# Up projection: rounded weights' products ahead of the remainders', no column shift of its weights, and 74 remainders built by ACT and an accumulating transfer that POOL issues

## The chip, the cores and the metric

The kernel runs on one core of one Trainium2 chip. The metric is the device time of one execution in microseconds (us), median of several runs. The engines are named as in the profile: PE (TensorE, matmuls), PEld (TensorE's weight loads, which run beside the matmuls), DVE (VectorE), ACT (ScalarE), POOL (GpSimd) and SP (SyncE, which issues most transfers).

## The reference

Two layers of a bidirectional encoder over 256 tokens of width 2048. The part that the change touches is the feed-forward half of a layer:

```
h2 = rms_norm(x, ln2_g[l])
u = depthwise_conv(h2 @ w_up[l], conv_w[l], conv_b[l])   # w_up: 2048 x 11264, conv over 3 positions
gate, up = u[..., :D_FF], u[..., D_FF:]                  # D_FF = 5632
x = x + (jax.nn.silu(gate) * up) @ w_down[l]
```

Ahead of it stand a projection of 2048 to 4608 columns, two kinds of attention and an output projection. All is in float32.

## The kernel before, in words

**Numbers in two parts.** A float32 product is made of three products of a shorter format (fp32r) that PE takes at full rate. A weight w is split by `split` (L109): ACT rounds it into `whi` (L112), and DVE subtracts, w - whi, into the remainder `wlo` (L113). The tokens are split in the same way into `xs[k]`, a tile of 2 x 256 columns with the rounded tokens in the first 256 and their remainders in the last 256. One long matmul of 512 columns, whi against both parts of `xs[k]`, gives two of the products; one short matmul of 256 columns, wlo against the rounded tokens alone, gives the third. The product of the two remainders is left out.

**The up projection.** Here the weights are the stationary operand (128 x 128, loaded anew for every matmul) and the tokens are the moving one. For each of the 44 groups `f` of 128 gate and 128 up columns the 16 slices `k` of 128 rows are summed in PSUM. The weights of a group come as two quanta `u` of 1 MB (128 x 2048), each worked in two half blocks of 128 x 1024. A half block holds 4 slices k for both sides j (gate and up), so it has 8 pairs of a long and a short matmul. `q_up` (L527) goes over j and k and calls `two` (L411), which issues the long matmul and at once the short one of the same pair. Two layers have 2 x 44 x 4 = 352 half blocks and 2816 pairs.

**Everywhere else** (input projection, output projection, down projection) the roles are swapped: tokens or activations are stationary, `whi` and `wlo` move with 512 columns, and `three` or `q_seven` issue the matmuls. Part of the down projection (kind "seven") uses a scheme with seven products, and its weights get some additions on DVE before they are split.

**Places in SBUF.** A tile `const` of 48 columns, `SHIFT`, sets where all later tiles begin. The tiles `whi` and `wlo` are 1024 + 64 columns wide; the up projection's weights lie in them from column 56 on (`UP_AT`, L53 and L756), all others from column 0. By the built program all of `xs`, `mid` (activations), `whi` and `wlo` begin at 96 bytes past a multiple of 256 bytes. So for the up projection the weights stand 224 bytes out of line with the tokens, and everywhere else the two are in line.

**What sets the order.** The work is a list of quanta. `load` (L735, its transfer is issued at L741) brings a quantum's raw weights by SP into one of three `raw` buffers; the next load into a buffer is issued when its last half was split. `split_w` (L752) splits a half block four steps ahead of its use (SPLIT_AHEAD), into one of five pairs of buffers. So the split of a half block can begin when the one five steps ahead of it has been multiplied, and it has four half blocks of time. A list scheduler then places the instructions of each engine; splits have a raised priority.

After a group's last half block `glu` (L543 to L563) takes the sums out of PSUM and makes the convolution, the gate and the product: on ACT L545, L555, L559, on DVE L546, L547, L557, L561, on POOL two copies of a halo (L549, L550), and then a split of the result into `mid` (L112, L113). For the seven products `sums_mid` adds more of it.

Of the kernel before, what the change touches and what calls it, by code (L numbers as in the profile page):

```python
# [12 lines left out]
F32R = mybir.dt.float32r  # L13
I32 = mybir.dt.int32
AF = mybir.ActivationFunctionType
ALU = mybir.AluOpType
AX = mybir.AxisListType

P = 128
# [4 lines left out]
KD = D // P  # L24
# [24 lines left out]
SPLIT_AHEAD = 4  # L49
AHEAD_PRIO = 40  # L50
SHIFT = 48

UP_AT = 56  # L53
WARM = 14

SPARE = 3 * (("qT", 3),)
# [3 lines left out]
def encoder_kernel(  # L60
# [5 lines left out]
    nc = tc.nc  # L66
    const = ctx.enter_context(tc.tile_pool(name="const", bufs=1))
    wp = ctx.enter_context(tc.tile_pool(name="wp", bufs=2))
# [28 lines left out]
    def mm(ps, lhsT, rhs, start, stop):  # L97
        nc.tensor.matmul(ps, lhsT, rhs, start=start, stop=stop, skip_group_check=True)  # L98
# [27 lines left out]
    xs = {}  # L126
# [276 lines left out]


    quanta = []
    side = {}

    def at(q, f, *args, half=1):
        side.setdefault((q, half), []).append((f, args))

    def two(ps, w_h, w_l, mv, first, last):  # L411

        mm(ps, w_h, mv, first, False)
        mm(ps[:, 1], w_l, mv[:, 0], False, last)

    def three(ps, terms, hv, lv, first, last, apart=False):

# [16 lines left out]
    def q_win(l, j, u):  # L434
        def body(q, half, hi, lo):
            ps = banks("in", u == 0 and half == 0)
            hv, lv = (w.rearrange("p (k n) -> p k n", k=2) for w in (hi, lo))
            k = 4 * u + 2 * half
            three(ps, (xs[k], xs[k + 1]), hv, lv, k == 0, k == KD - 2)
            if half == 0:  # L440
                return
            if u == 0 and j == 0 and l > 0:
                load_qk_g(l)
            if u == 2 and j == 1:
                rope_tables(l)
            if u == 3:
                if l == 0 and j == 0:
                    at(q + 4, done_win, q, l, j, ps, half=0)
                else:
                    done_win(q, l, j, ps)  # L450
        return body
# [38 lines left out]
    def q_wout(l, grp, nb, u):  # L490
        def body(q, half, hi, lo):
            g = 0 if grp == "a" else 1
            ps = banks("out", u == 0 and half == 0)
            hv, lv = (w.rearrange("p (k n) -> p k n", k=2) for w in (hi, lo))
            h = 4 * u + 2 * half
            three(ps, (os[g * NH + h], os[g * NH + h + 1]), hv, lv, h == 0, h == NH - 2)
            if nb == 0 and u == 0 and half == 1:
                stat_o(grp)
            if u == 1 and half == 1:
                if grp == "b":  # L500
                    add_x(nb, ps, st["ro"])
                else:
                    whole_x(q, l, 1, nb, ps, st["ro"])
        return body
# [22 lines left out]
    def q_up(l, f, u):  # L527
        def body(q, half, hi, lo):
            if u == 0 and half == 0:
                cur["up"] = psum.tile([P, 2, 2, T], F32, name="mm", bufs=2)  # L530
            ps = cur["up"]
            hv, lv = (w.rearrange("p (k j n) -> p k j n", k=4, j=2) for w in (hi, lo))
            for j in range(2):
                for kk in range(4):
                    k = 8 * u + 4 * half + kk
                    two(ps[:, j], hv[:, kk, j], lv[:, kk, j], xs[k], k == 0, k == KD - 1)
            if u == 1 and half == 1:
                glu(l, f, ps)
        return body

    def glu(l, f, ps):
        ux = halo[f % 2]
        r = T // GRID_W  # L543
        t = work.tile([P, 2, T], F32, name="prob", bufs=2)
        nc.scalar.activation(t, ps[:, :, 0], AF.Copy)  # L545
        nc.vector.tensor_add(t, t, ps[:, :, 1])  # L546
        nc.vector.tensor_mul(ux[:, :, r:r + T], t, st["r2"][:, None, :].to_broadcast([P, 2, T]))  # L547

        nc.gpsimd.tensor_copy(ux[:, :, 1:r], ux[:, :, T:T + r - 1])  # L549
        nc.gpsimd.tensor_copy(ux[:, :, T + r:T + 2 * r - 1], ux[:, :, r + 1:2 * r])  # L550
        y = work.tile([P, 2, T], F32, name="pT", bufs=4)
        for j in range(2):
            c = j * NF + f
            w0, w1, w2, b = (par["conv"][:, l, i, c:c + 1] for i in range(4))
            nc.scalar.activation(y[:, j, :], ux[:, j, r:r + T], AF.Identity, scale=w1, bias=b)  # L555
            for w, o in ((w0, 0), (w2, 2 * r)):
                nc.vector.scalar_tensor_tensor(y[:, j, :], ux[:, j, o:o + T], w, y[:, j, :],  # L557
                                               op0=ALU.mult, op1=ALU.add)
        nc.scalar.activation(t[:, 0, :], y[:, 0, :], AF.Silu)  # L559
        m = work.tile([P, T], F32, name="bias", bufs=2)  # L560
        nc.vector.tensor_mul(m, t[:, 0, :], y[:, 1, :])  # L561
        gs[f] = middle(l, f)
        split(gs[f][:, 0], gs[f][:, 1], m)  # L563
        ms[f] = m
        if f % 2 and f < NF - CHUNKS[-1] + PART:
            sums_mid(l, f // 2, ms.pop(f - 1), ms.pop(f))
# [132 lines left out]
    for l in range(L):  # L699
        for j in range(NJ):  # L700
            for u in range(4):
                quanta.append((a["w_in"][l, j, u], q_win(l, j, u), ""))
        for grp in "ba":
            for nb in range(NB):
                for u in range(2):
                    quanta.append((a["w_out"][l, 0 if grp == "a" else 1, nb, u], q_wout(l, grp, nb, u), ""))
        f = 0
        for c, nf in enumerate(CHUNKS):
            up = lambda f: [(a["w_up"][l, f, u], q_up(l, f, u), "up") for u in range(2)]
            down = lambda nb, g: [(a["w_down"][l, sum(CHUNKS[:c]) // FG + g, nb], q_down(l, c, nb, g), "")]  # L710
            seven = lambda i: [(a["w_seven"][l, c, i], q_seven(l, c, i), "seven")]

            end = sum(CHUNKS[:c]) + PART + 1
            while f < end:
                quanta += up(f)
                f += 1
            quanta.append((a["w_plain"][l, c], q_plain(l, c), ""))
            if nf == PART:
                for i in range(PAIRS):
                    quanta += seven(i) + down(2 + i // 2, i % 2)  # L720
            else:

                for i in range(PAIRS):
                    quanta += seven(i)
                    if f < NF:
                        quanta += up(f)
                        f += 1
                for nb, g in ((2, 0), (2, 1), (2, 2), (0, 2), (3, 0), (1, 2), (3, 1), (3, 2)):
                    quanta += down(nb, g)


    steps = [(q, h) for q in range(len(quanta)) for h in range(3 if quanta[q][2] == "seven" else 2)]
    raw, hl, left, loads, highs = {}, {}, {}, {}, {}

    def load(q, parts=1):  # L735
        if q < len(quanta):
# [6 lines left out]
    def split_seven(w, part, hi, lo):  # L743

        hv, lv = (t.rearrange("p (k n) -> p k n", k=2) for t in (hi, lo))
        if part == 1:
            nc.vector.tensor_sub(w[:, 1:3], w[:, 1:3], w[:, 2:4])
            nc.vector.tensor_add(w[:, 3], w[:, 3], w[:, 1])
            nc.vector.tensor_sub(w[:, 0], w[:, 3], w[:, 0])
        return split(hv, lv, (w[:, 1::2], w[:, 1:3], w[:, 0::3])[part])  # L750

    def split_w(s, parts=1):  # L752
        if s < len(steps):
            q, half = steps[s]
            kind = quanta[q][2]
            o = UP_AT if kind == "up" else 0  # L756
            hl[s] = tuple(wp.tile([P, 1024 + 64], F32R, name=t, bufs=SPLIT_AHEAD + 1)[:, o:o + 1024]
                          for t in ("whi", "wlo"))
            with tc.high_priority(offset=AHEAD_PRIO if s >= KD // 2 else 0):
                if kind == "seven":  # L760
                    highs[s] = split_seven(raw[q].rearrange("p (k n) -> p k n", k=4), half, *hl[s])
                else:
                    m = 1024 // parts
                    for j in range(parts):
                        highs[s] = split(*(t[:, j * m:(j + 1) * m] for t in hl[s]),
                                         raw[q][:, half * 1024 + j * m:half * 1024 + (j + 1) * m])
            left[q] -= 1
            if left[q] == 0:
                del raw[q]
                load(q + LOAD_AHEAD)  # L770
# [61 lines left out]
    ps = psum.tile([P, T], F32, name="pv", bufs=1)  # L832
# [3 lines left out]
    for i in range(SPLIT_AHEAD):  # L836
        first_x(i)
        split_w(i, 2 if i == 0 else 1)
# [122 lines left out]
```

## Time and profile before

| | |
|---|---|
| median of 3 runs | 2092.17 us (2092.07 to 2092.38) |
| the profiled execution: its time | 2092.0 us |
| its span | 2090.2 us |
| PE busy | 2083.5 us, 10816 matmuls |
| DVE busy | 1720.5 us |
| ACT busy | 1222.3 us |
| POOL busy | 170.3 us |
| moved by the transfers | 408.42 MB, 195 GB/s in the mean |

The profile is one execution with the start and the length of every instruction. Its page has, among others, the busy time of each engine, the chain of work that ended last (followed back from the end, at each step to what released it), and groups of like instructions with their count, their busy time and the mean of one. The timeline lists instructions in order of time; like ones that follow each other stand in one row with their count, and the time of such a row runs from the first one's start to the last one's end. Matmuls overlap: the next begins before the last has ended. So what one of them costs is read from start to start, not from its length.

### The profile page before, as it was taken

The page shows a single profiled execution, that of the slowest core. Times are in us where ns is not written, and L with a number is a line of the kernel's source. Part 1 is how long each engine was busy: PE and PEld are TensorE (multiplying, and loading weights), DVE is VectorE, ACT ScalarE, POOL GpSimd, SP SyncE. Part 2 cuts the span into 40 slices and gives each one's busy share as a digit, 9 for nine tenths or more (in the row PEclk, how much of TensorE's full clock was granted, in tenths as well). Part 3 has the DMA queues.
Part 4 walks back from the last instruction along what each step waited for, and adds up shares of the span by engine and source line. Part 5 has one row for each costly group of instructions (what it writes and reads, how often), then busy time and mean ns, then how long its engine had stood idle before and what let it go on. Part 6 is the DMA issues. An engine that isn't in the chain of part 4 may idle for free.

```text
span 2090.2 us, 29185 instructions
## 1 busy us (share of the span) xinstructions
PE 2083.5 (100%) x10816; PEld 1789.2 (86%) x10816; DVE 1720.5 (82%) x2604; ACT 1222.3 (58%) x1817; POOL 170.3 (8%) x237
## 2 busy tenths in 40 slices
PE   9999999999999999999999999999999999999999
PEld 8888888888888888888888888888888888888887
DVE  7786757898898988989757866678989989899896
ACT  7566556555555556556555665565556555555563
POOL 0011100100101001010000011001001010010100
PEclk9999999999999999999999999999999999999999
DMA  9544555556565564655655444555555655556554
GB/s 350 199 145 164 179 172 174 198 195 211 180 241 182 208 210 167 242 193 211 208 181 181 162 160 166 177 182 189 214 202 170 236 199 204 201 185 234 185 200 161
DMA packets 62144, 408.42 MB, mean 195 GB/s; under 512 B 7344, under 2 KB 9904, under 8 KB 13744
## 3 DMA queue, kind: packets, MB, share of 16 engines
q1 hardware_dynamic: 61280, 405.46, 56.2%
q8 instruction: 85, 1.39, 0.3%
q10 hardware_dynamic: 720, 1.08, 0.2%
q14 instruction: 59, 0.48, 0.1%
HBM read 404.42 MB, written 2.10 MB: 194 GB/s over the span
## 4 chain that ended last, share of the span: by engine, by line
PE 99%; DMA 0%; ACT 0%; DVE 0%; issue 0%
PE mm L98 90%; PE S L98 4%; PE pv L98 3%; PE tr L98 2%; PE tr L373 1%; PE tr L307 1%; PE S L149 1%; DMA head<-in_head 0%; ACT qtok L274 0%; ACT kT L315 0%; ACT xs L115 0%; DVE x L688 0%; ACT whi L112 0%
## 5 line engine op out<-in xcount | busy, mean ns | idle before, releaser
L112 ACT ACTIVATE whi<-raw 128x1024 fp32r<-128x1024 f32 (+1 forms) x797 | 830.9, 1057 | 689.9 <-PE mm L98 411.9
L113 DVE TENSOR_TENSOR wlo<-raw,whi 128x1024 fp32r<-128x1024 f32 (+1 forms) x797 | 963.9, 1220 | 270.3 <-ACT whi L112 231.8
L98 PE MATMUL mm<-xs,whi 128*128 128x512 f32 x2816 | 977.0, 390 | 0.0
L98 PE MATMUL mm<-xs,wlo 128*128 128x256 f32 x2816 | 794.1, 282 | 0.0
L98 PEld LDWEIGHTS mm<-xs,whi 128*128 128x128 f32 x2816 | 528.3, 188 | 110.5
L98 PEld LDWEIGHTS mm<-xs,wlo 128*128 128x128 f32 x2816 | 532.2, 189 | 1.1
L98 PE MATMUL mm<-whi,mid 128*128 128x512 f32 x1412 | 368.2, 391 | 0.0
L98 PEld LDWEIGHTS mm<-whi,mid 128*128 128x128 f32 x1412 | 263.0, 188 | 53.9
L98 PE MATMUL mm<-whi,xs 128*128 128x512 f32 x1152 | 294.2, 393 | 1.4 <-ACT qtok L274 1.3
L98 PEld LDWEIGHTS mm<-whi,xs 128*128 128x128 f32 x1152 | 213.1, 188 | 44.7 <-ACT qtok L274 1.8
L98 PE MATMUL mm<-wlo,mid 128*128 128x512 f32 x706 | 202.4, 392 | 0.0
L98 PE MATMUL mm<-wlo,xs 128*128 128x512 f32 x576 | 159.5, 393 | 0.0
L98 PEld LDWEIGHTS mm<-wlo,mid 128*128 128x128 f32 x706 | 132.1, 188 | 27.0
L557 DVE SCALAR_TENSOR_TENSOR pT<-halo,conv,pT 128x256 f32<-128x256 f32 x352 | 148.1, 478 | 0.9
L549 POOL COPY halo<-halo 128x6 f32<-128x6 f32 x88 | 39.6, 450 | 1232.6 <-DVE halo L547 1232.6
L98 PEld LDWEIGHTS mm<-wlo,xs 128*128 128x128 f32 x576 | 107.3, 188 | 21.6
L555 ACT ACTIVATE pT<-halo,conv 128x256 f32<-128x256 f32 x176 | 95.1, 587 | 5.8 <-DVE halo L547 5.7
L550 POOL COPY halo<-halo 128x6 f32<-128x6 f32 x88 | 77.1, 876 | 0.2 <-POOL halo L549 0.2
L547 DVE TENSOR_TENSOR halo<-prob,acc_b 128x512 f32<-128x512 f32 x88 | 60.6, 689 | 1.9
L546 DVE TENSOR_TENSOR prob<-prob,mm 128x512 f32<-128x512 f32 x88 | 59.8, 679 | 0.0
L545 ACT ACTIVATE prob<-mm 128x512 f32<-128x512 f32 x88 | 51.3, 583 | 7.1 <-PE mm L98 7.1
L559 ACT ACTIVATE prob<-pT 128x256 f32<-128x256 f32 x88 | 35.5, 404 | 30.0 <-DVE pT L557 30.0
(180 smaller groups left out, 1475.4 us busy)
## 6 DMA issues: line engine op xcount, KB each, us to landing
raw<-in_w_up SPq DMA_DIRECT2D x176, 1024.0 KB, 4.9
raw<-in_w_in SPq DMA_DIRECT2D x71, 1024.0 KB, 4.9
raw<-in_w_down SPq DMA_DIRECT2D x48, 1024.0 KB, 4.8
raw<-in_w_seven SPq DMA_DIRECT2D x40, 1024.0 KB, 4.9
raw<-in_w_out SPq DMA_DIRECT2D x32, 1024.0 KB, 4.9
raw<-in_w_plain SPq DMA_DIRECT2D x10, 1024.0 KB, 4.8
bias<-in_bias SPq DMA_DIRECT2D x16, 160.0 KB, 3.1
x<-in_x SPq DMA_DIRECT2D x4, 512.0 KB, 10.7
```

Of the source, the lines that this page charges most:

```text
L98: nc.tensor.matmul(ps, lhsT, rhs, start=start, stop=stop, skip_group_check=True)
L112: high = nc.scalar.activation(hi, src, AF.Copy)
L113: nc.vector.tensor_sub(lo, src, hi.bitcast(F32))
L149: nc.tensor.transpose(ps[:, j, tt * P:(tt + 1) * P], x[:, tt, (k + j) * P:(k + j + 1) * P], ident)
L545: nc.scalar.activation(t, ps[:, :, 0], AF.Copy)
L546: nc.vector.tensor_add(t, t, ps[:, :, 1])
L547: nc.vector.tensor_mul(ux[:, :, r:r + T], t, st["r2"][:, None, :].to_broadcast([P, 2, T]))
L549: nc.gpsimd.tensor_copy(ux[:, :, 1:r], ux[:, :, T:T + r - 1])
L550: nc.gpsimd.tensor_copy(ux[:, :, T + r:T + 2 * r - 1], ux[:, :, r + 1:2 * r])
L555: nc.scalar.activation(y[:, j, :], ux[:, j, r:r + T], AF.Identity, scale=w1, bias=b)
L557: nc.vector.scalar_tensor_tensor(y[:, j, :], ux[:, j, o:o + T], w, y[:, j, :], op0=ALU.mult, op1=ALU.add)
L559: nc.scalar.activation(t[:, 0, :], y[:, 0, :], AF.Silu)
```

## The change

1. `two` takes the whole half block. It issues the eight long matmuls first, and then the eight short ones.
2. `UP_AT` goes, and the tiles `whi` and `wlo` are 1024 columns wide. The up projection's weights now begin at column 0 and are in line with the tokens, as all others.
3. In 74 half blocks the remainder is made otherwise. These are the last halves of a group (quantum u = 1, half 1), unless one of the five steps ahead is of the kind "seven". ACT writes the negated rounded weight into `wlo` (L772 of the kernel after), POOL issues a transfer that reads the same 512 KB of weights from memory once more and adds them onto `wlo` (L773), and ACT writes `whi` (L774). DVE has no part in it.

The diff, cut to its core:

```diff
-UP_AT = 56
 WARM = 14
...
+    second = set()
...
-    def two(ps, w_h, w_l, mv, first, last):
-
-        mm(ps, w_h, mv, first, False)
-        mm(ps[:, 1], w_l, mv[:, 0], False, last)
+    def two(terms):
+
+        for ps, w_h, w_l, mv, first, last in terms:
+            mm(ps, w_h, mv, first, False)
+        for ps, w_h, w_l, mv, first, last in terms:
+            mm(ps[:, 1], w_l, mv[:, 0], False, last)
...
-            for j in range(2):
-                for kk in range(4):
-                    k = 8 * u + 4 * half + kk
-                    two(ps[:, j], hv[:, kk, j], lv[:, kk, j], xs[k], k == 0, k == KD - 1)
+            two([(ps[:, j], hv[:, kk, j], lv[:, kk, j], xs[k], k == 0, k == KD - 1)
+                 for j in range(2) for kk, k in enumerate(range(8 * u + 4 * half, 8 * u + 4 * half + 4))])
...
-            up = lambda f: [(a["w_up"][l, f, u], q_up(l, f, u), "up") for u in range(2)]
+            def up(f):
+                second.add(len(quanta) + 1)
+                return [(a["w_up"][l, f, u], q_up(l, f, u), "up") for u in range(2)]
...
+    def added(s):
+
+        q, half = steps[s]
+        return half == 1 and q in second and not any(
+            quanta[steps[i][0]][2] == "seven" for i in range(s - SPLIT_AHEAD - 1, s))
...
-            o = UP_AT if kind == "up" else 0
-            hl[s] = tuple(wp.tile([P, 1024 + 64], F32R, name=t, bufs=SPLIT_AHEAD + 1)[:, o:o + 1024]
-                          for t in ("whi", "wlo"))
+            hl[s] = tuple(wp.tile([P, 1024], F32R, name=t, bufs=SPLIT_AHEAD + 1) for t in ("whi", "wlo"))
...
+                elif added(s):
+
+                    w = slice(half * 1024, (half + 1) * 1024)
+                    nc.scalar.activation(hl[s][1], raw[q][:, w], AF.Copy, scale=-1.0)
+                    nc.gpsimd.dma_start(out=hl[s][1], in_=quanta[q][0][:, w], accum_op=ALU.add)
+                    highs[s] = nc.scalar.activation(hl[s][0], raw[q][:, w], AF.Copy)
```

On PE, the first half block of the first up projection. Before, four of its eight pairs:

```order
L98 MATMUL mm<-xs_2795,whi 128x512
L98 MATMUL mm<-xs_2795,wlo 128x256
L98 MATMUL mm<-xs_2798,whi 128x512
L98 MATMUL mm<-xs_2798,wlo 128x256
L98 MATMUL mm<-xs_2806,whi 128x512
L98 MATMUL mm<-xs_2806,wlo 128x256
L98 MATMUL mm<-xs_2809,whi 128x512
L98 MATMUL mm<-xs_2809,wlo 128x256
```

The same half block after the change, from its fifth to its twelfth matmul:

```order
L96 MATMUL mm<-xs_2795,whi 128x512
L96 MATMUL mm<-xs_2798,whi 128x512
L96 MATMUL mm<-xs_2806,whi 128x512
L96 MATMUL mm<-xs_2809,whi 128x512
L96 MATMUL mm<-xs_2795,wlo 128x256
L96 MATMUL mm<-xs_2798,wlo 128x256
L96 MATMUL mm<-xs_2806,wlo 128x256
L96 MATMUL mm<-xs_2809,wlo 128x256
```

Long and short matmuls no longer alternate: a half block changes from long to short once, and the next one changes back.

On ACT, a stretch of the first layer's up projection around the split of a group's last half block. `whi_4793` is that half block's in the program before; `mid` is the split of the finished group, `prob` and `pT` belong to its gate. Before:

```order
L112 ACTIVATE whi_4773<-raw_4640 128x1024
L559 ACTIVATE prob_4700<-pT_4706 128x256
L112 ACTIVATE whi_4793<-raw_4640 128x1024
L112 ACTIVATE mid_4716<-bias_4714 128x256
L112 ACTIVATE mid_4724<-tq_4719 128x256
L112 ACTIVATE mid_4727<-tq_4719 128x256
L112 ACTIVATE whi_4834<-raw_4682 128x1024
```

The same stretch after the change, where that half block's tiles are `whi_4806` and `wlo_4807`:

```order
L110 ACTIVATE whi_4786<-raw_4652 128x1024
L558 ACTIVATE prob_4713<-pT_4719 128x256
L774 ACTIVATE whi_4806<-raw_4652 128x1024
L110 ACTIVATE mid_4729<-bias_4727 128x256
L772 ACTIVATE wlo_4807<-raw_4652 128x1024
L110 ACTIVATE mid_4737<-tq_4732 128x256
L110 ACTIVATE mid_4740<-tq_4732 128x256
L110 ACTIVATE whi_4848<-raw_4695 128x1024
```

The negated copy stands behind the rounded one and behind one split of `mid`; the other splits of `mid` come one instruction later.

On POOL, the start of the same up projection; `r1` is a root, `halo0` and `halo1` are the convolution's buffers. Before:

```order
L107 TENSOR_TENSOR r1_3131<-v_c2_3132,power_80 128x2
L549 COPY halo0_110<-halo0_110 128x2x3
L550 COPY halo0_110<-halo0_110 128x2x3
L549 COPY halo1_112<-halo1_112 128x2x3
L550 COPY halo1_112<-halo1_112 128x2x3
```

After:

```order
L773 DMA wlo_3041<-in_w_up 128x1024
L105 TENSOR_TENSOR r1_3132<-v_c2_3133,power_80 128x2
L773 DMA wlo_3164<-in_w_up 128x1024
L548 COPY halo0_110<-halo0_110 128x2x3
L549 COPY halo0_110<-halo0_110 128x2x3
L773 DMA wlo_3269<-in_w_up 128x1024
L548 COPY halo1_112<-halo1_112 128x2x3
L549 COPY halo1_112<-halo1_112 128x2x3
```

The transfers are queued on POOL between the halo copies, one ahead of each pair.

More of the change, by code (lines that the diff above doesn't have):

```diff
@@ L719, in encoder_kernel @@
                 for i in range(PAIRS):
-                    quanta += seven(i) + down(2 + i // 2, i % 2)
+                    quanta += seven(i)
+                    quanta += down(2 + i // 2, i % 2)
             else:
```

## The prediction

> **What bounds the kernel now.** I read the page's busy times first, then the chain of waits, then PE's own waits.
>
> ```profile
> span 2090.2 us, 29185 instructions
> PE 2083.5 (100%) x10816; PEld 1789.2 (86%) x10816; DVE 1720.5 (82%) x2604; ACT 1222.3 (58%) x1817; POOL 170.3 (8%) x237
> PE 99%; DMA 0%; ACT 0%; DVE 0%; issue 0%
> PE mm L98 <- ACT qtok L274: 1.3, 2, 0.7
> PE pv L98 <- DVE halfpi L94: 1.1, 1, 1.1
> ```
>
> PE is busy for 2083.5 of 2090.2 us, 99% of the chain that ended last is PE, and its waits for other engines come to 1.3 + 1.1 us. So no other engine can be sped up to any use: at most 6.7 us of idle PE time are there. A row of the windows view on a stretch that is mostly up projection shows none of it, beside a DVE that is 90% busy:
>
> ```profile
> 560.00:1040.00 480.00, 480.00 (x2531) 415.01 (x2530) 433.40 (x597) 283.38 (x387) 34.45 (x56) 1.00 0.59 205
> ```
>
> PE is busy in all 480.00 us, DVE in 433.40, and the granted clock is 1.00. What decides is therefore the rhythm in which PE takes its matmuls. The group rows say how many there are:
>
> ```profile
> L98 PE MATMUL mm<-xs,whi 128*128 128x512 f32 x2816 | 977.0, 390 | 0.0
> L98 PE MATMUL mm<-xs,wlo 128*128 128x256 f32 x2816 | 794.1, 282 | 0.0
> L112 ACT ACTIVATE whi<-raw 128x1024 fp32r<-128x1024 f32 (+1 forms) x797 | 830.9, 1057 | 689.9 <-PE mm L98 411.9
> L113 DVE TENSOR_TENSOR wlo<-raw,whi 128x1024 fp32r<-128x1024 f32 (+1 forms) x797 | 963.9, 1220 | 270.3 <-ACT whi L112 231.8
> ```
>
> Their lengths (390 and 282 ns) overlap, so I take starts from the timeline of PE, in the up projection:
>
> ```profile
> 900.14 0.39 PE L98 MATMUL mm<-xs,whi 128*128 128x512 f32 x1
> 900.37 0.28 PE L98 MATMUL mm<-xs,wlo 128*128 128x256 f32 x1
> 900.49 0.39 PE L98 MATMUL mm<-xs,whi 128*128 128x512 f32 x1
> ...
> 911.23 0.39 PE L98 MATMUL mm<-xs,whi 128*128 128x512 f32 x1
> ```
>
> From 900.14 to 911.23 lie 32 pairs: 11.09 / 32 = 0.3466 us a pair, some 0.23 for the long matmul and 0.12 for the short one, and 2.773 us for a half block of eight pairs. 2816 pairs make 976 us, near half the span.
>
> **Part 1, the rhythm (parts 1 and 2 of the change together).** No row of before has eight long matmuls and then eight short ones, but the pieces are in the trace, with operands in line as the change puts them. Long ones in a settled series, in the down projection:
>
> ```profile
> 579.82 1.52 PE L98 MATMUL mm<-whi,mid 128*128 128x512 f32 x6
> 581.18 0.62 PE L98 MATMUL tr<-whi,mid 128*128 128x512 f32 x2
> ```
>
> 581.18 - 579.82 = 1.36 for six: 0.2267 each. Short ones in a row, and long ones right behind them, stand in the attention of group B (scores, six matmuls of 256 columns, then the input projection), one place from each layer:
>
> ```profile
> 112.14 0.28 PE L98 MATMUL S<-kTb,qT 128*128 128x256 f32 x1
> ...
> 112.86 2.00 PE L98 MATMUL mm<-whi,xs 128*128 128x512 f32 x8
> 114.70 1.07 PE L98 MATMUL mm<-wlo,xs 128*128 128x512 f32 x4
> ...
> 1153.34 0.28 PE L98 MATMUL S<-kTb,qT 128*128 128x256 f32 x1
> 1153.45 0.28 PE L98 MATMUL S<-kTb,mid 128*128 128x256 f32 x1
> 1153.57 0.28 PE L98 MATMUL S<-mid,qT 128*128 128x256 f32 x1
> ...
> 1154.05 2.00 PE L98 MATMUL mm<-whi,xs 128*128 128x512 f32 x8
> 1155.89 0.39 PE L98 MATMUL mm<-wlo,xs 128*128 128x512 f32 x1
> ```
>
> Six short ones take 112.86 - 112.14 = 0.72 and 1154.05 - 1153.34 = 0.71, that is 0.119 each; the first is cheaper (0.11) and the next cost 0.12. Eight long ones behind them take 114.70 - 112.86 = 1.84 and 1155.89 - 1154.05 = 1.84, where eight settled ones take 8 x 0.2267 = 1.813. So a change from short to long costs some 0.027 us until the series has settled again. Before, the change of length is part of the steady alternation; after, each half block pays it once.
>
> A half block after: 8 x 0.119 + 1.84 = 0.953 + 1.84 = 2.793 us. Before: 2.773. That is 0.020 more in each of the 352 half blocks, **7.0 us**. I take this value because both pieces have the lengths, the order and the alignment that the change makes, twice with the same times.
>
> Its bounds. Below: if the long ones stay settled (1.813) and all short ones cost what the first did (0.11), a half block has 2.693, and the sum is 352 x -0.080 = -28 us. Above: the long ones that follow only two short ones are dearest,
>
> ```profile
> 100.66 0.40 PE L98 MATMUL S<-kTb,qT 128*128 128x256 f32 x2
> 100.89 0.40 PE L98 MATMUL mm<-wlo,xs 128*128 128x512 f32 x1
> 101.12 0.40 PE L98 MATMUL mm<-whi,xs 128*128 128x512 f32 x1
> 101.36 0.49 PE L307 MATMUL tr<-ident,qtok 128*128 128x128 f32 x3
> ```
>
> with 0.47 for two, 0.235 each. If all eight cost that and the short ones 0.12, a half block has 2.84, and the sum is 352 x 0.067 = +24 us.
>
> **Part 2, DVE's relief.** 74 subtractions of 1.22 us (L113) leave DVE, 90 us. It is worth nothing: PE never waits for DVE in the up projection. Where the seven products stand, the rule of the change spares no subtraction.
>
> **Part 3, ACT's extra copies.** 74 x 1.06 = 78 us more on ACT, which is 58% busy. Its row L112 has idle time ahead of it because it waits for PE to free a buffer, so the copies fall into idle time. Cover gone, they would cost at most 1.06 each.
>
> **Part 4, the transfer.** What happens now where the change puts it, from the timelines of ACT, of DVE and of POOL:
>
> ```profile
> 902.01 1.06 ACT L112 ACTIVATE whi<-raw 128x1024 fp32r<-128x1024 f32 x1 [1.42 <-PE mm L98]
> 902.98 0.40 ACT L112 ACTIVATE mid<-bias 128x256 fp32r<-128x256 f32 x1
> ```
>
> ```profile
> 901.47 0.42 DVE L561 TENSOR_TENSOR bias<-prob,pT 128x256 f32<-128x256 f32 x1
> ...
> 903.11 1.23 DVE L113 TENSOR_TENSOR wlo<-raw,whi 128x1024 fp32r<-128x1024 f32 x1 [0.24 <-ACT whi L112]
> ```
>
> ```profile
> 908.55 0.19 POOL L549 COPY halo<-halo 128x6 f32<-128x6 f32 x1 [9.71 <-DVE halo L547]
> ```
>
> At 902.01 PE frees the pair of buffers of a group's last half block. That half block is multiplied four half blocks later, 902.01 + 4 x 2.78 = 913.1, and its first short matmul comes after eight long ones, 1.84 later, at 914.9; that is what the new order buys. The rounded copy can start 0.95 earlier than now (its buffer is free when the long ones are done). The split of `mid` waits for DVE until 901.89 and then for that copy, until some 902.5; the negated copy ends at 903.6, and POOL can issue. This leaves 914.9 - 903.6 = 11.3 us. The nearest transfers:
>
> ```profile
> raw<-in_w_up SPq DMA_DIRECT2D x176, 1024.0 KB, 4.9
> x<-in_x SPq DMA_DIRECT2D x4, 512.0 KB, 10.7
> ```
>
> 1 MB lands in 4.9 us, and the slowest row of 512 KB, at the crowded start, has 10.7. Neither is issued by POOL nor adds to what is there, so the price is unknown; I take 5 to 8, nearer to the first since the queue is as loaded there as here, and count nothing. The bound below is 0 as well, since nothing can arrive before it is asked for. Behind the waiting issue on POOL stand the next group's halo copies, which DVE and ACT of `glu` wait for; they come at 908.55, some 5 us after the issue, and POOL has been idle for 9.71 us by then, so they aren't held up. SP's next load waits for the last reader of `raw`, now ACT's copy at 903.6 instead of a DVE subtraction at 904.3. The transfers read 74 x 0.5 MB more, a tenth of all.
>
> The Trainium skill, page "DMA: Bandwidth & Descriptors", section "Anatomy of one DMA", gives 2.0 us + bytes / 436e3 for a transfer that GpSimd issues; my estimate by it is 3.2 us for 512 KB, which would leave the sum as it is. No run here shows it yet.
>
> **Sum.** 7.0 + 0 + 0 + 0. The profiled execution took 2092.0 us (span 2090.2), 0.17 under the median of the runs; from the median, 2092.2 + 7.0 = **2099.2 us**. A measurement of this kernel can tell about 0.2% from no change, 4.2 us.
>
> **The rivals.**
>
> *No change (within 4.2 us).* A settled long matmul and a settled short one, 0.2267 + 0.12, come to 0.3467, the 0.3466 of the alternation. If the order doesn't matter at all, the time is 2092. Against it stands the 1.84 after short ones, seen both times. It would need the long series to settle within one or two matmuls. [...]
>
> *Faster.* The pieces in the attention alternate between operand tiles; in the up projection the short series may hold its cheap first step. With settled long ones (1.813) the half block is faster than now as soon as a short one costs under 0.120, and by more than 4.2 us under 0.118. At 0.115 it is 352 x (0.920 + 1.813 - 2.773) = -14 us, **2078**. For it: the 0.11 at 1153.34. Against it: the next steps cost 0.12, and the long series is not settled.
>
> *Much slower: the remainder comes late.* Place: the first short matmul of the 74 half blocks. It decides from 11.3 us between issue and landing; each us more costs up to 74 us. At 12.3 the time is 2099 + 74 = 2173. For it: an accumulating transfer has to read its target as well, and the 10.7 of 512 KB is near. Against it: 4.9 for twice the bytes. The Trainium skill, page "SBUF — State Buffer", section "Who interferes with whom", says that a transfer issued from GpSimd can be held up while DVE runs in a two-port mode. DVE's longest instruction here has 1.22 us, which the slack takes.
>
> *Never settled.* All long ones at 0.235: up to +24, 2116.
>
> **How the numbers follow.** Forecast 0.48 (its own range 2096.4 to 2104), no change 0.22, faster 0.15, remainder late 0.08, never settled 0.07. Faster than 2088: 0.15; within 0.2%: 0.22; slower: 0.63. The range 2086 to 2113 holds the forecast, no change, the upper edge of faster and most of never settled, some 0.8.
>
> **What would show it.** In the profile after: PE still busy in the whole up projection without waits for DMA; in a half block, 0.95 for the short and 1.84 for the long eight, with long steps of over 0.23 behind the change; DVE near 1630 us, ACT near 1300, 74 more transfers with a time to landing under 11. Wrong would be long ones at 0.2267 from the second on, short ones under 0.118, or PE waiting for a transfer at `wlo`.

## The result and the profile after

The kernel after takes 2098.94 us (median of 6 runs, 2098.91 to 2100.19) against 2092.16 us before (6 runs, 2091.99 to 2093.0): a ratio of 1.0033, with a 95% interval of 1.0022 to 1.0044. It is slower by 6.8 us; 7.0 were forecast. The profiled execution took 2098.92 us.

From the page of the kernel after, the span, the busy times, the chain, two of the groups and two rows of the transfers:

```profile
span 2097.1 us, 29429 instructions
PE 2089.9 (100%) x10816; PEld 1788.5 (85%) x10816; DVE 1632.5 (78%) x2522; ACT 1299.9 (62%) x1899; POOL 208.6 (10%) x319
...
PE 99%; DMA 0%; ACT 0%; ACTq 0%; DVE 0%; issue 0%
...
L111 DVE TENSOR_TENSOR wlo<-raw,whi 128x1024 fp32r<-128x1024 f32 (+1 forms) x715 | 865.2, 1222 | 276.9 <-ACT whi L110 210.2
...
L773 POOL DMA_DIRECT2D wlo<-in_w_up x82 | 71.7, 874 | 801.7 <-ACT wlo L772 594.3
...
raw<-in_w_up SPq DMA_DIRECT2D x176, 1024.0 KB, 5.7
...
wlo<-in_w_up POOLq DMA_DIRECT2D x82, 512.0 KB, 7.8
```

The span grew by 2097.1 - 2090.2 = 6.9 us and PE's busy time by 2089.9 - 2083.5 = 6.4. DVE lost 88 us of busy time and nothing came of it. The transfers are 82, not 74: on POOL they stand in 74 places, in eight of which two follow each other directly. So the number given with the change and in the prediction is too small by 8.

PE's waits after, by releaser (us in total, times, longest):

```profile
PE mm L96 <- ACT qtok L272: 1.3, 2, 0.7
PE pv L96 <- DVE halfpi L92: 1.1, 1, 1.1
PE mm L96 <- ACT whi L110: 0.3, 1, 0.3
```

No transfer is among them, and only the last row, 0.3 us at one place, is new. So the loss lies in matmuls that follow each other without a wait: summed from start to start, the up projection's matmuls take 983.4 us against 977.1 before, 6.3 of the 6.9. The same stretch of the windows view as before shows PE without a gap, and DVE with 406 in place of 433 us:

```profile
560.00:1040.00 480.00, 480.00 (x2521) 413.31 (x2520) 406.25 (x571) 304.28 (x405) 46.24 (x80) 1.00 0.73 229
```

PE's timeline in the up projection, where each row of eight runs from its first start to its last end:

```profile
901.01 1.11 PE L96 MATMUL mm<-xs,wlo 128*128 128x256 f32 x8
901.96 2.00 PE L96 MATMUL mm<-xs,whi 128*128 128x512 f32 x8
903.80 1.12 PE L96 MATMUL mm<-xs,wlo 128*128 128x256 f32 x8
904.75 1.55 PE L96 MATMUL mm<-xs,whi 128*128 128x512 f32 x6
```

From start to start: eight short ones 0.95, eight long ones 1.84, eight short ones 0.95. That is 2.79 a half block against 2.773 before. The median over all half blocks whose sixteen matmuls nothing interrupts, from the trace's starts, is 2.793; step by step (medians) the long ones cost 233, 236, 228, 232, 231 and three times 227 ns and the short ones 113, 119 and six times 120. This is the sequence of the attention's rows that the prediction put together. 352 x 0.020 = 7.0 us; the sum over all starts, 6.3, is a little less. Not every half block has this pattern: the scheduler sets the long ones of two half blocks side by side in eight places, and mixes the order at the start of each layer.

### The profile page after: what moved, and what is told of

Read it like the earlier page. It is cut to its first block, busy times and chain, and to the rows that moved or that the text cites. A ratio compares the mean times of both kernels' runs of the same rounds, so it can differ in the third digit from the quotient of the medians.

```text
span 2097.1 us, 29429 instructions
## 1 busy us (share of the span) xinstructions
PE 2089.9 (100%) x10816; PEld 1788.5 (85%) x10816; DVE 1632.5 (78%) x2522; ACT 1299.9 (62%) x1899; POOL 208.6 (10%) x319
## 4 chain that ended last, share of the span: by engine, by line
PE 99%; DMA 0%; ACT 0%; ACTq 0%; DVE 0%; issue 0%
PE mm L96 90%; PE S L96 4%; PE pv L96 3%; PE tr L96 2%; PE tr L371 1%; PE tr L305 1%; PE S L147 0%; DMA mid<-in_xT 0%; ACT qtok L272 0%; ACT kT L313 0%; ACT whi L110 0%; ACT xs L113 0%; DVE x L687 0%; ACTq L794 0%; ACTq L787 0%
## 5 line engine op out<-in xcount | busy, mean ns | idle before, releaser
L111 DVE TENSOR_TENSOR wlo<-raw,whi 128x1024 fp32r<-128x1024 f32 (+1 forms) x715 | 865.2, 1222 | 276.9 <-ACT whi L110 210.2
L110 ACT ACTIVATE whi<-raw 128x1024 fp32r<-128x1024 f32 (+1 forms) x715 | 744.2, 1056 | 520.0 <-PE mm L96 299.1
L96 PE MATMUL mm<-xs,whi 128*128 128x512 f32 x2816 | 704.0, 392 | 0.0
L96 PEld LDWEIGHTS mm<-xs,wlo 128*128 128x128 f32 x2816 | 383.3, 190 | 26.9
L96 PE MATMUL mm<-xs,wlo 128*128 128x256 f32 x2816 | 392.6, 282 | 0.0
L773 POOL DMA_DIRECT2D wlo<-in_w_up x82 | 71.7, 874 | 801.7 <-ACT wlo L772 594.3
L774 ACT ACTIVATE whi<-raw 128x1024 fp32r<-128x1024 f32 x82 | 86.8, 1059 | 88.0 <-PE mm L96 86.2
L548 POOL COPY halo<-halo 128x6 f32<-128x6 f32 x88 | 39.3, 447 | 476.9 <-DVE halo L546 476.9
L772 ACT ACTIVATE wlo<-raw 128x1024 fp32r<-128x1024 f32 x82 | 85.8, 1046 | 0.0
L111 DVE TENSOR_TENSOR mid<-bias,mid 128x256 fp32r<-128x256 f32 x82 | 34.7, 423 | 47.7 <-ACT mid L110 47.4
```

The costliest lines, as they stand in the source:

```text
L110: high = nc.scalar.activation(hi, src, AF.Copy)
L111: nc.vector.tensor_sub(lo, src, hi.bitcast(F32))
L772: nc.scalar.activation(hl[s][1], raw[q][:, w], AF.Copy, scale=-1.0)
L773: nc.gpsimd.dma_start(out=hl[s][1], in_=quanta[q][0][:, w], accum_op=ALU.add)
L774: highs[s] = nc.scalar.activation(hl[s][0], raw[q][:, w], AF.Copy)
```

## The experiments

Twelve kernels, each timed beside the kernel before. "Half block" is the median from start to start over the uninterrupted half blocks of each trace. "Order" is how long and short matmuls follow each other: alternating, or in groups of so many. "In" and "out" say whether the up projection's weights stand in line with the tokens or 56 columns (224 bytes) out of line.

| | order | whi | wlo | transfers | half block (us) | time (us) | ratio to before, 95% interval |
|---|---|---|---|---|---|---|---|
| before | alternating | out | out | none | 2.773 | 2092.2 | 1 |
| after | eights | in | in | 82 | 2.793 | 2098.9 | 1.0033, 1.0022 to 1.0044 |
| e1 | eights | out | out | none | 2.805 | 2103.9 | 1.0057, 1.0043 to 1.0071 |
| e2 | alternating | in | in | none | 2.830 | 2110.7 | 1.0088, 1.0075 to 1.0102 |
| e3 | eights | in | in | none | 2.793 | 2098.9 | 1.0032, 1.0019 to 1.0045 |
| e4 | alternating | out | out | 82 | 2.773 | 2101.2 | 1.0050, 1.0038 to 1.0063 |
| e5 | fours | in | in | none | 2.807 | 2104.0 | 1.0056, 1.0043 to 1.0069 |
| e6 | sixteens | in | in | none | 2.783 | 2101.6 | 1.0045, 1.0033 to 1.0058 |
| e7 | eights | in | in | 156 | 2.793 | 2108.1 | 1.0083, 1.0069 to 1.0097 |
| e8 | eights | in | out | none | 2.780 | 2094.1 | 1.0009, 1.0000 to 1.0018 |
| e9 | alternating | in | out | none | 2.827 | 2110.9 | 1.0089, 1.0075 to 1.0103 |
| e10 | alternating | out | in | none | 2.756 | 2086.3 | 0.9972, 0.9961 to 0.9983 |
| e11 | eights | in | out | 82 | 2.780 | 2093.9 | 1.0009, 1.0001 to 1.0018 |
| e12 | alternating | out by 48 | in | none | 2.720 | 2074.9 | 0.9917, 0.9903 to 0.9930 |

### One part of the change at a time: e1 to e4

**e1: the order alone.** The kernel before with `two(terms)` and the call in `q_up` from the change; `UP_AT` stays.

> The kernel before with the new order alone: eight long matmuls, then eight short ones; the up projection's weights stay 56 columns out of line with the tokens, and DVE makes all remainders. Theory (each change from short to long unsettles the series, and only in-line series settle at 0.2267 us): the eight long ones don't settle, 8 x 0.233 + 0.953 = 2.82 us a half block against 2.773, so 352 x 0.044 = +15 us, 2108 us. Rival 1 (the order alone costs, the place of the weights does not matter): 2.793 a half block as in the kernel after, 2099 us. Rival 2 (the order costs nothing, the lost shift does): 2092 us.

2103.94 us, half block 2.805 us. From PE's timeline:

```profile
900.05 1.10 PE L98 MATMUL mm<-xs,wlo 128*128 128x256 f32 x8
900.99 2.03 PE L98 MATMUL mm<-xs,whi 128*128 128x512 f32 x8
902.85 1.11 PE L98 MATMUL mm<-xs,wlo 128*128 128x256 f32 x8
903.79 2.03 PE L98 MATMUL mm<-xs,whi 128*128 128x512 f32 x8
```

Eight long ones take 902.85 - 900.99 = 1.86: out of line they never settle, as the theory has it. The short ones take 0.94, a little less than the 0.953 that the theory took from the in-line rows, and so it is +11.8 in place of +15. Both rivals are out, by 4.9 us and by 11.9.

**e2: the place alone.**

```diff
-UP_AT = 56
+UP_AT = 0
...
-            hl[s] = tuple(wp.tile([P, 1024 + 64], F32R, name=t, bufs=SPLIT_AHEAD + 1)[:, o:o + 1024]
+            hl[s] = tuple(wp.tile([P, 1024], F32R, name=t, bufs=SPLIT_AHEAD + 1)[:, o:o + 1024]
```

> The kernel before with the shift alone taken away: long and short matmuls alternate, weights in line with the tokens. Theory: every second matmul is a change from short to long, which in line has cost 0.234 and more for the long one and 0.114 to 0.118 for the short one behind it, 0.349 to 0.352 a pair against 0.3466, so +7 to +15 us, 2099 to 2107 us. Rival 1 (the place of the weights does not matter): 2092 us. Rival 2 (the lost shift is the whole loss): 2099 us.

2110.71 us, 3.7 above the theory's range of 2099 to 2107, and further above both rivals:

```profile
900.17 0.28 PE L98 MATMUL mm<-xs,wlo 128*128 128x256 f32 x1
900.28 0.40 PE L98 MATMUL mm<-xs,whi 128*128 128x512 f32 x1
900.52 0.28 PE L98 MATMUL mm<-xs,wlo 128*128 128x256 f32 x1
900.63 0.40 PE L98 MATMUL mm<-xs,whi 128*128 128x512 f32 x1
```

Long ones at 0.24, short ones at 0.11 (medians 0.236 and 0.118). So in the kernel before the shift is worth 18.6 us, and the new order is worth 11.8 us in line (e2 to e3) and costs 11.8 us out of line (before to e1). Order and place can't be priced apart from each other.

**e3: the kernel after without its transfers.**

```diff
-                elif added(s):
+                elif False:
```

> The kernel after without its transfers: order and place as in the kernel after, but DVE makes all remainders. Theory (the loss is PE's rhythm, the transfers are free): 2099 us, the same half block of 2.793 us. Rival (the transfers' traffic, or the copies on ACT, cost part of the 7 us): 2092 to 2097 us. Rival (the relief of DVE hides a loss that the order would bring without it): over 2100 us, with waits of PE for DVE.

2098.88 us, against 2098.94 with them, and the same half block. Taken together, the transfers, the copies on ACT and the relief of DVE are worth nothing in the kernel after, neither way. Both rivals fall.

**e4: the transfers alone.** The kernel after, with `two` issuing each short matmul right behind its long one, and with the 56 columns as before.

> The kernel before with the transfers alone: alternation and the shift of 56 columns stay, and in 82 half blocks the remainder comes by ACT and the transfer that POOL issues. The remainder is wanted with the first pair, 1.6 us earlier than in the kernel after, so some 9.5 us behind the issue; the landing took 7.5 to 10.7, median 7.8. Theory: 2092 to 2094 us, a few waits of PE of up to 1.2 us. Rival (the new order is what makes the transfers possible): PE waits in most of the 82, 0.5 to 1.5 us each, 2130 to 2200 us.

2101.16 us (2100.25 to 2107.56), 9 us above before, at the same half block of 2.773. The theory's 2094 is exceeded and the rival's 2130 not reached. The tile's view on POOL says who waits (us, times), and how long the transfers took. PE's waits lie within those of its weight loads (PEld), so the two don't add up:

```profile
who waited for it (us, times):
  PEld mm L96: 7.7, 10
  PE mm L96: 4.6, 8
...
DMA to landing us min/median/max: 7.6/7.9/10.6
```

and PE's timeline shows the longest of the matmuls' waits in its brackets:

```profile
776.72 0.38 PE L96 MATMUL mm<-xs,wlo 128*128 128x256 f32 x1 [1.73 <-DMA wlo<-in_w_up]
```

Most transfers arrive in time here as well, but not the slow ones: weight loads wait for 10 of the 82. Between the issue and the first load of the remainder lie 8.6 us in the median, and 10.8 in the kernel after. So this is what the new order buys: the 1.84 us ahead of the first short matmul. It saves the waits that only the transfers bring, 7.7 us in the profiled run and 9 in the median time, and with the change of place it costs 7.

### How often the length changes: e5 and e6

**e5: groups of four.** The call of `two` goes into a loop over j.

> The kernel after without transfers, in groups of four: four long matmuls, four short ones, for each side j, all in line. Twice as many changes of length. Theory A (each change from short to long costs the same 0.020 us net): 2 x 7 = +14 us on before, 2106 us. Theory B (what a change costs depends on whether the series before it had settled: four long ones don't settle, short ones behind them cost 0.117 to 0.118 as at 108.8 us in the trace of before, and the long ones behind those then take 0.235 once and 0.227 after): 916 + 471 ns for four pairs, 2.774 a half block, 2092 to 2094 us. Rival (the time has to do with the order of operands, not with the changes): 2099 us.

```profile
900.62 0.63 PE L96 MATMUL mm<-xs,wlo 128*128 128x256 f32 x4
901.09 1.09 PE L96 MATMUL mm<-xs,whi 128*128 128x512 f32 x4
902.02 0.64 PE L96 MATMUL mm<-xs,wlo 128*128 128x256 f32 x4
902.50 1.09 PE L96 MATMUL mm<-xs,whi 128*128 128x512 f32 x4
```

Four long ones take 902.02 - 901.09 = 0.93, four short ones 0.48; 2104.01 us. Theory B, with 2092 to 2094, falls: no group of long ones began with 0.235 and went on with 0.227. The rival's 2099 falls too. Theory A is nearer, 11.8 measured against 14: each group of four long ones (0.928 and 0.929 in the median) loses some 0.022 against four settled ones, where a group of eight loses 0.027.

**e6: groups of sixteen.** Half 0 issues its long ones and keeps its short ones for half 1:

```diff
+            for p2, w_h, w_l, mv, first, last in terms:
+                mm(p2, w_h, mv, first, False)
+            cur["late"] = terms if half == 0 else cur["late"] + terms
+            if half == 1:
+                for p2, w_h, w_l, mv, first, last in cur["late"]:
+                    mm(p2[:, 1], w_l, mv[:, 0], False, last)
```

> The kernel after without transfers, with the short matmuls of both half blocks of a quantum behind the long ones: 8 long, 8 long, 16 short. Half as many changes. Theory A and B alike: 1.841 + 1.813 + 0.232 + 14 x 0.120 = 5.566 us for two half blocks, 2.783 each, +3.5 us on before, 2095.7 us. Rival (long and short series cost what they cost, however many changes): 2099 us. The remainders' buffers are held longer, so PE might wait for DVE: more than 2099 us, with waits in the profile.

```profile
900.82 2.08 PE L96 MATMUL mm<-xs,wlo 128*128 128x256 f32 x16
902.73 3.82 PE L96 MATMUL mm<-xs,whi 128*128 128x512 f32 x16
906.39 2.08 PE L96 MATMUL mm<-xs,wlo 128*128 128x256 f32 x16
908.30 3.82 PE L96 MATMUL mm<-xs,whi 128*128 128x512 f32 x16
```

Sixteen short ones take 1.91, sixteen long ones 906.39 - 902.73 = 3.66: 5.57 for two half blocks, 2.783 each, as both theories said. The time, 2101.59 us, is 6 above their 2095.7. Summed over PE's starts, the up projection is 3.2 us longer than before, near the 3.5 expected, and some 5.6 more lie in the down projection's matmuls (`mm<-whi,mid` and `mm<-wlo,mid`), 2.0 of them in two waits for ACT (`pT`, L560). That the buffers held longer would make PE wait was expected as possible, for DVE; why these waits came is not shown.

### Twice the transfers: e7

```diff
-                second.add(len(quanta) + 1)
+                second.update((len(quanta), len(quanta) + 1))
```

> The kernel after with the transfer in the last half of both quanta of a group: 156 transfers instead of 82. Theory (a transfer that lands in time is free; median landing 7.8 us against 11.2 us of time): 2099 us, DVE some 90 us less busy, no waits of PE for them, the landing 8 to 9 us. Rival (the traffic delays each other and the raw loads): landings over 11 us, PE waits, over 2105 us.

2108.12 us (2105.78 to 2114.78), with the median half block unchanged. The tile's view on POOL, and a row of the transfers:

```profile
who waited for it (us, times):
  PEld mm L96: 10.7, 14
  PE mm L96: 5.3, 8
...
DMA to landing us min/median/max: 8.2/9.8/12.3
...
raw<-in_w_up SPq DMA_DIRECT2D x176, 1024.0 KB, 8.6
```

The rival holds for the slow transfers: the median landing is 9.8 us in place of 7.8, 20 of the 156 take over the 11 us there are, the slowest 12.3, and weight loads wait in 14 places, the matmuls themselves in 8 of these. The raw loads take 8.6 us in place of 5.7. The 82 transfers of the kernel after are free only because they are few.

### Where the weights stand: e8 to e12

**e8: only the remainders out of line, in eights, without transfers.**

```diff
-            hl[s] = tuple(wp.tile([P, 1024], F32R, name=t, bufs=SPLIT_AHEAD + 1) for t in ("whi", "wlo"))
+            hl[s] = tuple(wp.tile([P, 1024 + 64], F32R, name=t, bufs=SPLIT_AHEAD + 1)[:, o:o + 1024]
+                          for t, o in (("whi", 0), ("wlo", 56 if kind == "up" else 0)))
```

> The kernel after without transfers, where only the remainders' tiles stand 56 columns out of line in the up projection; the rounded weights stay in line. Theory (it is the settled in-line short series of 0.120 that unsettles the long one behind it; out of line the short ones cost 0.117): 8 x 0.117 + 0.235 + 7 x 0.227 = 2.760 us a half block against 2.773, 352 x -0.013 = -4.6 us, 2087.6 us. Rival (any change from short to long unsettles an in-line series for five matmuls): 0.936 + 1.841 = 2.777, +1.4 us, 2093.6 us. Rival 2 (out-of-line short ones unsettle it for longer, as the attention's values did, whose tiles are 64 bytes off): 0.936 + 1.850 = 2.786, 2096.7 us.

2094.05 us. From PE's timeline:

```profile
901.71 1.10 PE L96 MATMUL mm<-xs,wlo 128*128 128x256 f32 x8
902.65 2.01 PE L96 MATMUL mm<-xs,whi 128*128 128x512 f32 x8
904.49 1.10 PE L96 MATMUL mm<-xs,wlo 128*128 128x256 f32 x8
```

The half block of 2.780 is that of the first rival (2.777): the short ones are cheaper, 0.94 for eight here and 0.93 in the median, and the long series is unsettled all the same, 1.85 in the median (steps 232, 236, 228, 232, 231, 227, 227, 235). So a change from short to long unsettles an in-line series whatever the short ones cost. The eighth long one, beside which the first out-of-line remainder is loaded, costs 235 ns; in e3, where that remainder is in line, it costs 227.

**e11: the same with the transfers.**

> The kernel after, transfers too, with the remainders' tiles alone out of line in the up projection. Theory (order, place and transfers add up, and the transfers land in time): the half block of 2.780 us as without transfers, 2094 us. Rival (the transfers, landing at another place, or the shorter long series leave PE waiting): over 2097 us.

2093.9 us, and no transfer among PE's waits. The rival falls. One shift in a single tile takes 5 of the change's 7 us back.

**e9 and e10: alternating, one of the two tiles out of line.** In the kernel before, the shift is 0 for `whi` and 56 for `wlo` (e9), or the reverse (e10):

```diff
-            hl[s] = tuple(wp.tile([P, 1024 + 64], F32R, name=t, bufs=SPLIT_AHEAD + 1)[:, o:o + 1024]
-                          for t in ("whi", "wlo"))
+            hl[s] = tuple(wp.tile([P, 1024 + 64], F32R, name=t, bufs=SPLIT_AHEAD + 1)[:, o:o + 1024]
+                          for t, o in (("whi", o), ("wlo", 0)))
```

> The kernel before (long and short alternate, DVE makes all remainders), with the remainders' tiles alone out of line; the rounded weights are put in line. Theory (alternation is cheap only where both stand out of line by the same 56 columns, so that the rhythm closes on itself): a long matmul beside the load of an out-of-line remainder 0.235, a short one beside the load of an in-line weight 0.113 to 0.120, 2.78 to 2.84 us a half block, 2096 to 2115 us. Rival (an out-of-line remainder's load costs a settled long series nothing, and short ones are cheaper beside it): 0.227 + 0.116, 2.744 a half block, -10 us, 2082 us: a version that beats both.

> The kernel before with the rounded weights alone out of line; the remainders' tiles are put in line. Theory: a long matmul beside the load of an in-line remainder, behind a short one, 0.234, a short one beside the load of an out-of-line weight 0.118, 2.816 a half block, +15 us, 2107 us. Rival (what matters is the place of the weight that the long matmul uses): 2092 us.

e9 has 2110.91 us, within the theory's range, though the steps differ: two kinds of pairs take turns, 231 and 117 ns, 235 and 124. e10 has 2086.34, where the theory said 2107 and the rival 2092: it is 5.8 us faster than the kernel before. From e10's timeline, two starts that lie 32 pairs apart:

```profile
900.01 0.39 PE L98 MATMUL mm<-xs,whi 128*128 128x512 f32 x1
...
911.03 0.39 PE L98 MATMUL mm<-xs,whi 128*128 128x512 f32 x1
```

That is 11.02 / 32 = 0.344 a pair. The theory that alternation is cheap only with both tiles out of line by the same amount falls.

**e12: e10 with 48 columns in place of 56.**

> The faster kernel of the run before (alternation, rounded weights alone out of line), with 48 columns in place of 56: 192 bytes out of line instead of 224. Theory (it matters that the two tiles differ in their place, not by how much): 2086 us, 2.756 us a half block. Rival (the amount matters as much as the fact): 3 us and more away from it, on either side.

2074.91 us, 17.3 us faster than before (ratio 0.9917, 0.9903 to 0.9930), the fastest of all. The theory's 2086 falls and the rival holds: the amount matters, 11.4 us between 56 columns and 48. From PE's timeline:

```profile
900.19 0.39 PE L98 MATMUL mm<-xs,whi 128*128 128x512 f32 x1
900.41 0.28 PE L98 MATMUL mm<-xs,wlo 128*128 128x256 f32 x1
900.53 0.39 PE L98 MATMUL mm<-xs,whi 128*128 128x512 f32 x1
...
911.07 0.39 PE L98 MATMUL mm<-xs,whi 128*128 128x512 f32 x1
```

32 pairs in 911.07 - 900.19 = 10.88, 0.340 a pair: every long one costs the settled 0.227 and every short one 0.113, the price that in the kernels with groups in line only the first short one behind a settled series has. Other amounts were not tried.

## Why the prediction was right

**The bound.** PE is busy without a wait over the stretch from 560 to 1040 us, before and after; e3, where DVE makes all the remainders again, has the same time to 0.1 us.

**The rhythm, 7.0 us.** Right in its size and in its steps: 0.953 and 1.84 forecast, 0.95 and 1.84 measured. It was right because the pieces were taken from places with the same lengths, the same order and the same alignment (by the built program the attention's tiles `kTb` and `qT` too begin at 96 bytes past a multiple of 256). The prediction did not know what order and place cost by themselves, and did not need to: e1 and e2 show 11.8 and 18.6 us for one without the other. e5 and e6 confirm that the change of length is what costs, in line: 2.807, 2.793 and 2.783 us a half block with four, eight and sixteen in a group.

**DVE's relief, nothing.** Right: 88 us less busy time on DVE, and the time of e3. **ACT's copies, nothing.** Right: ACT went up by 77.6 us to 1299.9, beside PE. The count was off (82, not 74), on terms whose price was nothing. That the forecast of 90 us for DVE and 78 for ACT fits even so is luck: 82 subtractions of 1.22 us make 100, but busy time counts instructions that overlap only once (before, DVE's lengths add up to 1866 us and its busy time to 1720.5), and the two errors nearly cancel.

**The transfer, nothing.** Right, by a thin margin that can be read in the trace. ACT's and POOL's timelines of the kernel after:

```profile
904.06 1.06 ACT L774 ACTIVATE whi<-raw 128x1024 fp32r<-128x1024 f32 x1 [1.44 <-PE mm L96]
905.02 0.40 ACT L110 ACTIVATE mid<-bias 128x256 fp32r<-128x256 f32 x1
905.33 1.04 ACT L772 ACTIVATE wlo<-raw 128x1024 fp32r<-128x1024 f32 x1
```

```profile
906.78 0.89 POOL L773 DMA_DIRECT2D wlo<-in_w_up  x1 [7.03 <-ACT mid L110]
```

and PE's, where this half block's short matmuls begin:

```profile
917.77 1.11 PE L96 MATMUL mm<-xs,wlo 128*128 128x256 f32 x8
```

The negated copy ends at 905.33 + 1.04 = 906.37, 11.4 us ahead of the first short matmul, where 11.3 were forecast. The issue comes 0.4 us behind it and leaves 917.77 - 906.78 = 11.0, and the landing takes this long (tile's view on POOL):

```profile
DMA to landing us min/median/max: 7.5/7.8/10.7
```

The slowest landed 0.4 us before the load of its weights began; the next closest had 1.0 us. The forecast weighed a typical landing, and that the slowest fits as well is luck in part. The estimate of 3.2 us by the Trainium skill's page "DMA: Bandwidth & Descriptors", section "Anatomy of one DMA", is under half of the measured 7.8. The forecast's "5 to 8", taken from this case's own rows, holds for the median of 7.8, but not for the slowest. That the order buys the transfers their time was right too; without it they cost 9 us (e4), and twice as many cost 9 us in spite of it (e7).

**The rivals.** "No change" failed since the long series does not settle at once. "Faster" failed since only the first short one has the cheap step. "Remainder late" needed longer landings, which e7 has, or less time for them, as in e4. "Never settled" is what e1 shows, for weights out of line.

**What stays open.** Why the place of the loaded weights against the moving tokens sets the rhythm is not settled by these runs. They show that it does, for the long and the short series and for the tile of each. e10 and e12 went against the theory of the time, and no new one was tried. Only 0, 192 and 224 bytes were tried, so that places repeat every 256 bytes is taken for granted and not shown.

## What to carry to other kernels

Where PE is busy throughout, read its rhythm from start to start, and price a new order of matmuls from stretches of the same trace with the same lengths, order and alignment; eight matmuls of a kind are not eight times one. Where weights are loaded for every matmul, try the places of each tile by itself and not of all together: here that was worth more than any other edit, 17.3 us. Work moved from an engine that nobody waits for is worth nothing, and a transfer that takes its place is free only while its slowest landing is ahead of its use.

## What the runs showed of the hardware that was not expected

One and the same alternation of 512 and 256 columns takes 0.354 us a pair with both tiles in line (2.830 / 8), 0.347 with both 224 bytes out, 0.345 with the long ones' weights alone 224 bytes out, and 0.340 with these 192 bytes out: 4% of the up projection for a place in memory. The page "SBUF — State Buffer" of the Trainium skill, section "Who interferes with whom", is about contention between engines; it gives PE two independent read ports, one for the moving operand and one for the weight loads, and says that PE never waits on anyone. In the stretches read above PE has no such wait here either, but the time of a matmul depends on where the weights that are loaded beside it lie: 235 ns for the eighth long one of e8 against 227 in e3.

An accumulating transfer of 512 KB that POOL issues takes 7.8 us to land, where a plain one of 1 MB by SP takes 5.7 beside it and 4.9 in the kernel before. How much of this is the adding and how much the issue by POOL no run separates.
